# A hybrid decoder layer: another order of additions, weightings, splits and squares around the norm ahead of w_up

## The chip, the cores and the metric

The kernel runs on one core of one Trainium2 chip. A core has TensorE (PE, matrix products into PSUM), VectorE (DVE), ScalarE (ACT), GpSimd (POOL) and SyncE (SP, which here only issues DMAs); each runs its own instructions in order, and semaphores tie them together. The metric is the device time of one execution in microseconds (us). Before the change it is 1495.16 us, the median of three runs (1495.01 to 1495.42).

## The reference, cut to what matters

One decoder layer on 256 tokens of width 2048, in float32. Only the second half of the first residual and the start of the MLP are touched:

```
mix = hybrid_mixer(rmsnorm(h, norm_mix_pre), ...)      # ends in  y_mix @ w_out
h   = h + rmsnorm(mix, norm_mix_post)
ff  = squared_relu_mlp(rmsnorm(h, norm_mlp_pre), w_up, w_down)
h   = h + rmsnorm(ff, norm_mlp_post)

rmsnorm(x, w)               = x * rsqrt(mean(x * x) + EPS) * w
squared_relu_mlp(u, wu, wd) = (relu(u @ wu) ** 2) @ wd
```

## The kernel before, in words

**Precision.** Every float32 operand of a product is split into a high part `hi`, rounded on ScalarE, and a low part `lo`, the rest, on VectorE (`split`, L135, with its two instructions L138 and L139). A product is then three matmuls: high by high, high by low, low by high (L815 to L817).

**Tiles.** Tokens stand in two tiles of 128, t = 0 and 1. Output columns go in blocks of 512. A unit of work covers two column blocks, b = 0 and 1, and so four PSUM accumulators. Weights come in groups: a `Group` (L774) holds two blocks of 128 rows by 1024 columns, fetched by SyncE (L784) into `raw` (four buffers) or `raw_p` (two), split into `hi`/`lo` (five buffers, `hl_tiles`, L665) or, each sixth time, `hi_p`/`lo_p`. `plain` (L808) multiplies a group: six matmuls for each row block and token tile. `advance` (L843) keeps fetching two groups and splitting ahead of the matmuls. Other groups (`seven`, L819) use seven products instead of eight and need sums of blocks of the activations: `sums` (L710) builds them on VectorE (L707 to L715) and splits them.

**Order.** From L922 on the order is written out by hand: each engine does its work in the order of the code.

**The stretch around the norm.** The last unit of w_out ends with three groups, `x_`, `y_`, `z_`, whose products are done first for token tile 0, then for tile 1. The residual and the norms are worked in between, and the first three groups of w_up, `g0`, `g1`, `g2` (`lead`), fill TensorE. The fourth group of w_up (called `g3` in the text) is the first one of the loop at L1082. In this stretch:

- `final(r, acc, t, b)` (L885, VectorE) completes a block of `mix`: `r0[t, b]` holds columns 0 and 1, `r1[t, b]` columns 2 and 3.
- `squared` (L891, ScalarE) squares it, and sums the squares into `ssq`.
- `weighted(r, n)` (L894, VectorE) multiplies by the norm's weights, in place, after the square has read the block.
- `scale_of(rm, t, ...)` gathers the sums (L903, L905, VectorE) and takes the power -0.5 on GpSimd (L906) into `rm`, the tile `rmix` of the profile.
- `last_of(t, b)` (L993) calls these for `r1`. For b = 1 the weighting is a multiplication on GpSimd (L1000).
- `sum_up(t, n)` (L966, VectorE) is the addition `h = h + r * rm` for block n of tile t; I write it (t,n). For n = 0, 1 the profile shows it as `m<-r,rmix,m`, for n = 2, 3 as `m<-m,rmix`.
- `turn(t, n)` (L972, TensorE) transposes four 128x128 pieces of that block into PSUM.
- `split_turned(t, n)` copies them with the weights of the MLP norm on ScalarE (L978, four instructions), casts (L980) and takes the rest (L981) on VectorE. The result is the activation of two groups of w_up: block 0 feeds g0 and g1, block 1 feeds g2 and g3, and so on. Its scratch `v` comes from `strip` (tag `uu`, two buffers), as that of `sums` and of `square_sums` does.
- `square_sums(t)` (L983) squares the four blocks of `h` on ScalarE (L985), reduces (L987, L989, VectorE), takes the power on GpSimd (L990) into `rmlp`, and stores `h` to memory from GpSimd's queue (L991).

The 1/rms of the MLP norm is not applied before the products but after them: `up_end` (L1066) scales by `rmlp` when a unit of w_up is complete. The stored `h` is read back in the last unit of w_down (`load_h`, L947).

Of the kernel before, what the change touches and what calls it, by code (L numbers as in the profile page):

```python
# [19 lines left out]
NT = S // P  # L20
# [22 lines left out]
AHEAD = 1_000_000  # L43
BUFS = 5
EARLY = 5
LATE = 3
# [25 lines left out]
def hymba_layer(ctx: ExitStack, tc: tile.TileContext, x, norm_mix_pre, w_in, conv_w, conv_b, dt_bias, a_log,  # L72
                d_skip, ssm_norm_w, w_out, norm_mix_post, norm_mlp_pre, w_up, w_down, norm_mlp_post,
                consts, out):
    nc = tc.nc
# [76 lines left out]
    def parts():  # L152
        return [wp.tile([P, KB, NB], F32R, name=n, bufs=BUFS) for n in ("hi", "lo")]
# [415 lines left out]
    for hb in range(2):  # L569
# [4 lines left out]
        for xb in (2 * hb, 2 * hb + 1):  # L574
            xT = conv_block(COL_X + xb * NB, 4 * xb)
            z = gate_block(COL_Z + xb * NB)
            for j in range(2):
                g = 2 * xb + j
# [63 lines left out]
    rm = cp.tile([P, NT], F32, name="rmix")  # L642
# [3 lines left out]
    def columns(n):  # L646
        return slice(n * NB, (n + 1) * NB)
# [17 lines left out]
    def hl_tiles():  # L665
        turns["hl"] += 1
        if turns["hl"] % (BUFS + 1):
            return parts()
        return [pp.tile([P, KB, NB], F32R, name=n) for n in ("hi_p", "lo_p")]

    def strip(dtype=F32):
        return pp.tile([P, NB], dtype, name="uu", tag="uu", bufs=2)

    def quarters(t):
        return t.rearrange("p (i s) -> p i s", s=P)
# [95 lines left out]
    def aside():  # L771
        return [pp.tile([P, 3, NB], F32R, name=n) for n in ("xh", "xl")]
# [58 lines left out]
    groups = []  # L831

    def plan(src, n, kind, order):
        first = len(groups)
        groups.extend(Group(src, n, kind(abs(k)), by_seven) for k, by_seven in order)
        return range(first, len(groups))

    def order_of(ks, by_seven):
        return [(k, k in by_seven) for k in ks]
# [3 lines left out]
    def advance(to, sums=True):  # L843

        with tc.high_priority(offset=AHEAD):
            for what, last in (("fetch", to + 2), ("divide", to), ("add", to + 1), ("sums", to + 1)):
                while at[what] <= min(last, len(groups) - 1):
                    g = groups[at[what]]
                    if what == "divide" and at["add"] == at["divide"]:
                        g.add()  # L850
                        at["add"] += 1
                    if what == "sums":
                        if g.by_seven:
                            g.acts.sums()
                    else:
                        getattr(g, what)()
                    at[what] += 1

    def run(unit, acc, more, combine=None, hooks={}, to=None, started=False):

        sevens = [i for i in unit if groups[i].by_seven]
        for i in unit[:to]:
            advance(i + 2)
            if i in sevens:
                groups[i].seven(acc, more, i == sevens[0], i == sevens[-1])
            else:
                groups[i].plain(acc, first=i == unit[0] and not started, last=i == unit[-1])
            if sevens and i == sevens[-1]:
                combine(more)
            if i - unit[0] in hooks:  # L870
                hooks[i - unit[0]]()
# [12 lines left out]
    def final(r, acc, t, b):  # L884
        nc.vector.tensor_tensor(r[t, b], acc[b + 2 * t], r[t, b], op=ALU.subtract if b else ALU.add)  # L885

    def four():
        return {(t, b): pp.tile([P, NB], F32, name="r", bufs=4) for t in range(NT) for b in range(2)}

    def squared(r, acc, t, b, n):  # L890
        nc.scalar.activation(acc[b + 2 * t], r, AF.Square, accum_out=ssq[:, t, n:n + 1])  # L891

    def weighted(r, n):
        nc.vector.tensor_mul(r, r, wpost[:, n])  # L894
# [6 lines left out]
    def scale_of(dst, t, some):  # L901
        v = cp.tile([P, 1], F32, name="mean", bufs=2)
        nc.vector.tensor_scalar(v, ssq[:, t, 2:3], some, None, op0=ALU.add)  # L903
        m = cp.tile([P, 1], F32, name="mean", bufs=2)
        nc.vector.tensor_scalar(m, ssq[:, t, 3:4], v, 1.0 / D, op0=ALU.add, op1=ALU.mult)  # L905
        nc.gpsimd.tensor_tensor(dst[:, t:t + 1], m, half[:, 0:1], op=ALU.pow)  # L906

    def load_wpost(pool, src):
# [6 lines left out]
    up = [plan(w_up, 2 * n, Pre,  # L915
               order_of(range(8), ()) if n == 0 else
               order_of((0, 1, 3, 2, 5, 4, 7, 6), (3, 5, 7)) if n < 7 else
               order_of((0, 1, 3, 2, 5, 4, 6, 7), (3, 5))) for n in range(8)]
# [16 lines left out]
    some = {}  # L935
    run(wo0, acc, more, combined(r0), {len(wo0) - 1: first_end}, started=True)
    acc, more = more, acc
    r1 = {}
# [18 lines left out]
    wpost = None  # L957
# [6 lines left out]
    def sum_up(t, n):  # L964
        r = (r0, r1)[n // 2][t, n % 2]
        nc.vector.scalar_tensor_tensor(h[t][:, columns(n)], r, rm[:, t:t + 1], h[t][:, columns(n)],  # L966
                                       op0=ALU.mult, op1=ALU.add)

    def turn(t, n):
        for f in range(4):  # L970
            k = 4 * n + f
            nc.tensor.transpose(more[n][:, f * P:(f + 1) * P], h[t][:, k * P:(k + 1) * P], ident)  # L972

    def split_turned(t, n):
        v = quarters(strip())
        for f in range(4):
            k = 4 * n + f
            nc.scalar.activation(v[:, f], more[n][:, f * P:(f + 1) * P], AF.Copy, scale=w_mlp[:, k:k + 1])  # L978
        hi, lo = (us[n][:, :, i, t * P:(t + 1) * P] for i in range(2))
        nc.vector.tensor_copy(hi, v)  # L980
        nc.vector.tensor_tensor(lo, v, hi.bitcast(F32), op=ALU.subtract)  # L981

    def square_sums(t):  # L983
        for n in range(4):
            nc.scalar.activation(strip(BF16), h[t][:, columns(n)], AF.Square, accum_out=ssh[:, t, n:n + 1])  # L985
        v = cp.tile([P, 1], F32, name="some", bufs=4)
        nc.vector.tensor_reduce(v, ssh[:, t], axis=mybir.AxisListType.X, op=ALU.add)  # L987
        m = cp.tile([P, 1], F32, name="mean", bufs=2)
        nc.vector.tensor_scalar(m, v, D * EPS, 1.0 / D, op0=ALU.add, op1=ALU.mult)  # L989
        nc.gpsimd.tensor_tensor(rmlp[:, t:t + 1], m, half[:, 0:1], op=ALU.pow)  # L990
        nc.gpsimd.dma_start(hd[:, t], h[t])  # L991

    def last_of(t, b):  # L993
        final(r1, acc, t, b)
        squared(r1[t, b], acc, t, b, 2 + b)
        if b == 0:
            weighted(r1[t, b], 2)
            return
        scale_of(rm, t, some[t])
        nc.gpsimd.tensor_mul(r1[t, b], r1[t, b], wpost[:, 3])  # L1000

    lead = up[0][:LATE]
    x_, y_, z_ = (groups[i] for i in late)
    g0, g1, g2 = (groups[i] for i in lead)
    advance(late[-1])
    with tc.high_priority(offset=AHEAD):
        g0.part(0, [v[:, 0:KB] for v in aside()])
    for b in range(2):
        for g in (x_, y_, z_):
            g.plain(acc, last=g is z_, ts=(0,), bs=(b,))  # L1010
        last_of(0, b)
    sum_up(0, 0)
    sum_up(0, 1)
    x_.plain(acc, ts=(1,))
    advance(lead[0])
    y_.plain(acc, ts=(1,))
    turn(0, 0)
    turn(0, 1)
    sum_up(0, 2)
    with tc.high_priority(offset=AHEAD):  # L1020
        g1.part(0, hl_tiles())
    split_turned(0, 0)
    z_.plain(acc, last=True, ts=(1,))
    advance(lead[1])
# [1 line left out]
    g0.plain(acc, first=True, ts=(0,))  # L1026
    for b in range(2):
        last_of(1, b)
    turn(0, 2)
    g1.plain(acc, ts=(0,))  # L1030
    sum_up(0, 3)
    sum_up(1, 0)
    sum_up(1, 1)
    turn(1, 0)
    with tc.high_priority(offset=AHEAD):
        g2.part(0, hl_tiles())
    split_turned(1, 0)
    turn(1, 1)
    turn(0, 3)
    split_turned(0, 2)  # L1040
    g0.plain(acc, first=True, ts=(1,))
    split_turned(1, 1)
# [1 line left out]
    sum_up(1, 2)  # L1044
    g1.plain(acc, ts=(1,))
    turn(1, 2)
    split_turned(0, 3)
    sum_up(1, 3)
    g2.plain(acc, ts=(0,))
    turn(1, 3)  # L1050
    split_turned(1, 2)
    g2.plain(acc, ts=(1,))
    split_turned(1, 3)
    for t in range(NT):
        square_sums(t)

    ending = deque()

    def up_end(r, acc, n):

        def end():
            for t in range(NT):
                for b in range(2):
                    if n:
                        final(r, acc, t, b)
                    nc.scalar.activation(r[t, b], r[t, b] if n else acc[b + 2 * t], AF.Relu, scale=rmlp[:, t:t + 1])  # L1066
                    nc.scalar.activation(r[t, b], r[t, b], AF.Square)
            ending.append((r, acc, n))
        return end
# [12 lines left out]
    for n in range(8):  # L1082
        r = four()
        unit = up[n] if n else up[0][LATE:]
        hooks = {len(unit) - 1: up_end(r, acc, n)}
        if n:
            hooks[1] = turned
        else:
            hooks.update({i: Pre(k).sums for i, k in ((0, 3), (1, 5), (2, 7))})
        run(unit, acc, more, combined(r), hooks, started=n == 0)  # L1090
        acc, more = more, acc

# [63 lines left out]
```

## Time and profile before

| what | value |
|---|---|
| median of three runs | 1495.16 us (1495.01 to 1495.42) |
| the profiled execution's own time | 1493.86 us |
| its span | 1491.8 us |
| its mean granted TensorE clock | 0.995 |
| stretch from 758 to 900 us: TensorE busy | 133.69 of 142.00 us, clock 0.98 |
| stretch from 500 to 700 us: TensorE busy | 199.12 of 200.00 us, clock 1.00 |
| stretch from 900 to 1300 us: TensorE busy | 400.00 of 400.00 us, clock 1.00 |
| DMA | 287.28 MB, mean 193 GB/s |

The span runs from the first to the last instruction of the profiled execution; its own time has 2.1 us more around it. A row of a timeline gives the start, the duration, the engine, the line, the operation, the tiles (out<-in), the shapes and the count, and in brackets the idle time before it with what ended that. Rows of matmuls overlap: they are pipelined, so their starts tell the pace, not their durations. `PEld` is TensorE's loading of weights, `issue` a wait that the profile can't attribute.

### The profile page before, as it was taken

How to read it: one execution, taken by the hardware profiler on the slowest of the kernel's cores; microseconds unless marked ns; L12 is line 12 of the kernel's file. 1: busy time of each engine (PE TensorE's matmuls, PEld its weight loads, DVE VectorE, ACT ScalarE, POOL GpSimd, SP SyncE). 2: the span in 40 equal slices, each digit the busy share in tenths (PEclk: the TensorE clock that was granted, in tenths of full speed). 3: DMA queues.
4: the chain of work that ended last, by engine and by line, in shares of the span. 5: the costliest groups of instructions: out<-in, count | busy, mean ns of one | idle time of the engine just before them, and what ended most of it. 6: DMA issues, size and time to landing. Idle time of an engine off the chain costs nothing. (4 is left out here: it accounts for less than half of the span.)

```text
span 1491.8 us, 19561 instructions
## 1 busy us (share of the span) xinstructions
PE 1471.1 (99%) x7229; PEld 1242.0 (83%) x7229; DVE 1157.7 (78%) x1609; ACT 845.2 (57%) x1138; POOL 54.1 (4%) x77
## 2 busy tenths in 40 slices
PE   9999999999999999999997999999999999999997
PEld 8888888888888888878885888888888888888886
DVE  6988897886555555597987778888887899779995
ACT  7574565455545454554556565676665665656462
POOL 0002100220000000000001000000000000000000
PEclk9999999999999999999999999999999999999998
DMA  7666666555656555555674555655555556657652
GB/s 270 203 201 181 182 185 186 182 169 169 175 167 182 169 170 176 190 169 205 247 238 176 187 176 211 211 186 187 197 182 193 199 196 216 221 186 259 219 188 96
DMA packets 108751, 287.28 MB, mean 193 GB/s; under 512 B 11392, under 2 KB 14320, under 8 KB 107632
## 3 DMA queue, kind: packets, MB, share of 16 engines
q1 hardware_dynamic: 103632, 272.37, 56.2%
q0 software_dynamic: 1152, 8.39, 1.6%
q10 hardware_dynamic: 3872, 5.28, 1.1%
q8 instruction: 56, 0.92, 0.3%
q14 instruction: 39, 0.32, 0.1%
HBM read 281.78 MB, written 4.23 MB: 192 GB/s over the span
## 5 line engine op out<-in xcount | busy, mean ns | idle before, releaser
L139 DVE TENSOR_TENSOR lo<-raw,hi 128x1024 fp32r<-128x1024 f32 (+1 forms) x367 | 447.9, 1224 | 181.6 <-ACT hi L138 180.8
L138 ACT ACTIVATE hi<-raw 128x1024 fp32r<-128x1024 f32 (+1 forms) x367 | 383.7, 1050 | 278.1 <-PE acc L221 108.5
L221 PE MATMUL acc<-q,hi 128*128 128x512 f32 x1024 | 283.3, 402 | 0.6 <-DVE q L141 0.6
L221 PEld LDWEIGHTS acc<-q,hi 128*128 128x128 f32 x1024 | 178.8, 189 | 27.3 <-DVE q L141 0.8
L817 PE MATMUL acc<-hi,q 128*128 128x512 f32 x472 | 183.7, 389 | 0.0
L815 PE MATMUL acc<-hi,q 128*128 128x512 f32 x472 | 183.6, 389 | 0.0
L816 PE MATMUL acc<-lo,q 128*128 128x512 f32 x472 | 183.6, 389 | 0.0
L224 PEld LDWEIGHTS acc<-q,lo 128*128 128x128 f32 x1024 | 152.9, 189 | 19.2
L224 PE MATMUL acc<-q,lo 128*128 128x256 f32 x1024 | 157.8, 281 | 0.0
L139 DVE TENSOR_TENSOR lo<-raw_p,hi 128x1024 fp32r<-128x1024 f32 x95 | 115.8, 1219 | 16.3 <-ACT hi L138 16.2
L138 ACT ACTIVATE hi<-raw_p 128x1024 fp32r<-128x1024 f32 x95 | 99.7, 1050 | 33.3 <-DVE raw_p L793 15.0
L816 PEld LDWEIGHTS acc<-lo,q 128*128 128x128 f32 x472 | 88.6, 188 | 18.5
L817 PEld LDWEIGHTS acc<-hi,q 128*128 128x128 f32 x472 | 88.6, 188 | 18.5
L815 PEld LDWEIGHTS acc<-hi,q 128*128 128x128 f32 x472 | 88.6, 188 | 18.3
L199 PE MATMUL acc<-hi,q 128*128 128x512 f32 x256 | 100.1, 391 | 0.0
L200 PE MATMUL acc<-lo,q 128*128 128x512 f32 x256 | 99.7, 389 | 0.0
L201 PE MATMUL acc<-hi,q 128*128 128x512 f32 x256 | 99.7, 389 | 0.0
L138 ACT ACTIVATE q<-uu 128x512 fp32r<-128x512 f32 x21 | 13.3, 632 | 132.9 <-DVE uu L715 132.9
L139 DVE TENSOR_TENSOR xl<-xr,xh 128x1536 fp32r<-128x1536 f32 x44 | 77.3, 1757 | 11.2 <-ACT xh L138 11.0
L138 ACT ACTIVATE xh<-xr 128x1536 fp32r<-128x1536 f32 x44 | 65.1, 1480 | 15.3 <-PE ps L829 7.5
L139 DVE TENSOR_TENSOR lo_p<-raw,hi_p 128x1024 fp32r<-128x1024 f32 x43 | 52.5, 1220 | 12.8 <-ACT hi_p L138 12.8
L815 PE MATMUL ps<-hi,q 128*128 128x512 f32 x152 | 59.5, 392 | 0.0
(361 smaller groups left out, 2565.3 us busy)
## 6 DMA issues: line engine op xcount, KB each, us to landing
raw<-in_w_in_dram SPq DMA_DIRECT2D x190, 512.0 KB, 3.6
raw<-in_w_up_dram SPq DMA_DIRECT2D x86, 512.0 KB, 4.5
raw<-in_w_down_dram SPq DMA_DIRECT2D x85, 512.0 KB, 5.1
raw<-in_w_out_dram SPq DMA_DIRECT2D x46, 512.0 KB, 4.0
raw_p<-in_w_down_dram SPq DMA_DIRECT2D x43, 512.0 KB, 5.1
raw_p<-in_w_up_dram SPq DMA_DIRECT2D x42, 512.0 KB, 4.6
raw_p<-in_w_out_dram SPq DMA_DIRECT2D x18, 512.0 KB, 5.1
bc<-acs_d ACTq DMA_DIRECT2D x8, 512.0 KB, 4.6
```

The source lines that it names most:

```text
L138: return (nc.scalar.activation(hi, src, AF.Copy), nc.vector.tensor_tensor(lo, src, hi.bitcast(F32), op=ALU.subtract))
L139: nc.vector.tensor_tensor(lo, src, hi.bitcast(F32), op=ALU.subtract))
L199: nc.tensor.matmul(acc[t], a_h[:, r, ts], hi[:, j], start=begin, stop=False)
L200: nc.tensor.matmul(acc[t], a_h[:, r, ts], lo[:, j], start=False, stop=False)
L201: nc.tensor.matmul(acc[t], a_l[:, r, ts], hi[:, j], start=False, stop=end)
L221: nc.tensor.matmul(acc[f], hi[:, j, f * P:(f + 1) * P], u(k0 + j), start=k0 + j == 0, stop=False, skip_group_check=True)
L224: nc.tensor.matmul(acc[f][:, 0], lo[:, j, f * P:(f + 1) * P], u(k0 + j)[:, 0], start=False, stop=k0 + j == NK - 1, skip_group_check=True)
L815: nc.tensor.matmul(a, a_h, hi[:, b], start=first and j == 0, stop=False)
L816: nc.tensor.matmul(a, a_h, lo[:, b], start=False, stop=False)
L817: nc.tensor.matmul(a, a_l, hi[:, b], start=False, stop=last and j == KB - 1)
```

## The change

All of it stands in the hand-written stretch. `last_of` now holds only the final and the square. The weighting of `r1[t, 1]` goes from GpSimd to VectorE: for tile 0 behind the split of g0's second half, for tile 1 far later, ahead of the addition (1,3). For tile 1 both finals and squares come ahead of the weighting and the scale; the additions (0,3), (1,0) and (1,1) move up in the code. The split of g2's first half goes behind the cast of block (1,0). The two splits of g3 go from the loop into the stretch, ahead of the blocks (1,2) and (1,3). `square_sums` goes from the stretch into the loop, tile 0 behind the second group there and tile 1 behind the third, each followed by `Pre(k).sums` as before.

```diff
@@ -993,11 +993,6 @@
     def last_of(t, b):
         final(r1, acc, t, b)
         squared(r1[t, b], acc, t, b, 2 + b)
-        if b == 0:
-            weighted(r1[t, b], 2)
-            return
-        scale_of(rm, t, some[t])
-        nc.gpsimd.tensor_mul(r1[t, b], r1[t, b], wpost[:, 3])
 
     lead = up[0][:LATE]
     x_, y_, z_ = (groups[i] for i in late)
@@ -1005,20 +1000,27 @@
     advance(late[-1])
     with tc.high_priority(offset=AHEAD):
         g0.part(0, [v[:, 0:KB] for v in aside()])
+    def ahead(g, j):
+        with tc.high_priority(offset=AHEAD):
+            g.part(j, hl_tiles())
+
     for b in range(2):
         for g in (x_, y_, z_):
             g.plain(acc, last=g is z_, ts=(0,), bs=(b,))
         last_of(0, b)
+        if b == 0:
+            weighted(r1[0, 0], 2)
+    scale_of(rm, 0, some[0])
     sum_up(0, 0)
     sum_up(0, 1)
     x_.plain(acc, ts=(1,))
     advance(lead[0])
+    weighted(r1[0, 1], 3)
     y_.plain(acc, ts=(1,))
     turn(0, 0)
     turn(0, 1)
     sum_up(0, 2)
-    with tc.high_priority(offset=AHEAD):
-        g1.part(0, hl_tiles())
+    ahead(g1, 0)
     split_turned(0, 0)
     z_.plain(acc, last=True, ts=(1,))
     advance(lead[1])
@@ -1026,17 +1028,18 @@
     g0.plain(acc, first=True, ts=(0,))
     for b in range(2):
         last_of(1, b)
+    weighted(r1[1, 0], 2)
+    scale_of(rm, 1, some[1])
+    sum_up(0, 3)
+    sum_up(1, 0)
     turn(0, 2)
     g1.plain(acc, ts=(0,))
-    sum_up(0, 3)
-    sum_up(1, 0)
+    turn(1, 0)
     sum_up(1, 1)
-    turn(1, 0)
-    with tc.high_priority(offset=AHEAD):
-        g2.part(0, hl_tiles())
+    turn(1, 1)
     split_turned(1, 0)
-    turn(1, 1)
     turn(0, 3)
+    ahead(g2, 0)
     split_turned(0, 2)
     g0.plain(acc, first=True, ts=(1,))
     split_turned(1, 1)
@@ -1044,15 +1047,17 @@
     sum_up(1, 2)
     g1.plain(acc, ts=(1,))
     turn(1, 2)
+    weighted(r1[1, 1], 3)
+    sum_up(1, 3)
     split_turned(0, 3)
-    sum_up(1, 3)
     g2.plain(acc, ts=(0,))
     turn(1, 3)
+    g3 = groups[up[0][LATE]]
+    ahead(g3, 0)
     split_turned(1, 2)
+    ahead(g3, 1)
     g2.plain(acc, ts=(1,))
     split_turned(1, 3)
-    for t in range(NT):
-        square_sums(t)
 
     ending = deque()
 
@@ -1086,7 +1091,8 @@
         if n:
             hooks[1] = turned
         else:
-            hooks.update({i: Pre(k).sums for i, k in ((0, 3), (1, 5), (2, 7))})
+            hooks.update({0: Pre(3).sums, 1: lambda: (square_sums(0), Pre(5).sums()),
+                          2: lambda: (square_sums(1), Pre(7).sums())})
         run(unit, acc, more, combined(r), hooks, started=n == 0)
         acc, more = more, acc
```

VectorE, around the sums of squares of the second token tile (L885 is the final, L894 the weighting, L903 and L905 the sums, L966 the additions, L980 and L981 the cast and the rest, L139 a split of weights), as the difference of the two orders:

```order
 L885 TENSOR_TENSOR m<-ps,m 128x512
+L885 TENSOR_TENSOR m<-acc,m 128x512
 L894 TENSOR_TENSOR m<-m 128x512
-L885 TENSOR_TENSOR m<-acc,m 128x512
 L903 TENSOR_SCALAR mean<-ssq,some 128x1
 L905 TENSOR_SCALAR mean<-ssq,mean 128x1
 L966 SCALAR_TENSOR_TENSOR m<-m,rmix 128x512
 L966 SCALAR_TENSOR_TENSOR m<-r,rmix,m 128x512 x2
+L980 CAST q<-uu 128x4x128
+L981 TENSOR_TENSOR q<-uu,q 128x4x128
 L139 TENSOR_TENSOR lo<-raw,hi 128x1024
```

The second final stands ahead of the first weighting, and the cast and the rest of block (1,0) ahead of the split of g2.

ScalarE, from the last two squares of `r1` to the first difference for `seven` (L978 are the copies of transposed blocks, L985 the squares for the MLP norm, L138 splits, `m<-uu` that of a difference), before the change:

```order
L891 ACTIVATE acc,ssq<-m 128x512
L138 ACTIVATE hi<-raw 128x1024
L978 ACTIVATE uu<-acc,par 128x128 x12
L138 ACTIVATE hi<-raw_p 128x1024
L978 ACTIVATE uu<-acc,par 128x128 x12
L985 ACTIVATE uu,ssh<-m 128x512 x8
L138 ACTIVATE hi_p<-raw 128x1024
L138 ACTIVATE hi<-raw 128x1024
L138 ACTIVATE hi<-raw_p 128x1024
```

The same engine from the same instruction on, with the change:

```order
L891 ACTIVATE acc,ssq<-m 128x512
L978 ACTIVATE uu<-acc,par 128x128 x4
L138 ACTIVATE hi<-raw 128x1024
L978 ACTIVATE uu<-acc,par 128x128 x8
L138 ACTIVATE hi<-raw_p 128x1024
L978 ACTIVATE uu<-acc,par 128x128 x4
L138 ACTIVATE hi_p<-raw 128x1024
L978 ACTIVATE uu<-acc,par 128x128 x4
L138 ACTIVATE hi<-raw 128x1024
L978 ACTIVATE uu<-acc,par 128x128 x4
L138 ACTIVATE hi<-raw_p 128x1024
```

The eight squares are gone from this place, and g3's splits (`hi_p`, then `hi`) stand between the copies. And the squares' new place on ScalarE, with the change:

```order
L138 ACTIVATE m<-uu 128x512
L138 ACTIVATE hi_p<-raw 128x1024
L138 ACTIVATE hi<-raw 128x1024
L985 ACTIVATE uu,ssh<-m 128x512 x4
L138 ACTIVATE m<-uu 128x512
L138 ACTIVATE hi<-raw_p 128x1024
L138 ACTIVATE hi<-raw 128x1024
L985 ACTIVATE uu,ssh<-m 128x512 x4
L138 ACTIVATE m<-uu 128x512
```

Four squares follow each of two pairs of splits and precede the split of a difference. The orders of TensorE's and of SyncE's instructions are the same as before.

## The prediction

> **What bounds the kernel now.** I read the page first, then TensorE's waits, then the stages around them, then the timelines there. On the page, a row gives an engine's busy time, its share and its instructions.
>
> ```profile
> PE 1471.1 (99%) x7229; PEld 1242.0 (83%) x7229; DVE 1157.7 (78%) x1609; ACT 845.2 (57%) x1138; POOL 54.1 (4%) x77
> ```
>
> TensorE is the bound, and its work does not change. Only its gaps and its clock can be won. Its two longest waits (total, times, longest):
>
> ```profile
> PE ps L815 <- ACT hi_p L138: 4.5, 1, 4.5
> PE acc L972 <- DVE m L966: 2.7, 1, 2.7
> ```
>
> Both lie in the edited stretch. I call the 2.7 wait A and the 4.5 wait B. The windows around them give busy times, granted clock and DMA:
>
> ```profile
> 787.00:794.00 7.00, 3.64 (x20) 2.56 (x20) 6.15 (x8) 3.77 (x14) 2.10 (x2) 1.00 0.20 60
> 804.40:815.10 10.70, 5.75 (x13) 4.09 (x13) 6.73 (x10) 9.30 (x18) 2.22 (x4) 0.69 0.68 253
> ```
>
> Around A the clock stays at 1.00; after B it falls to 0.69, so B costs more than its length. B on TensorE, and what comes behind it:
>
> ```profile
> 803.91 0.39 PE L816 MATMUL acc<-lo,q 128*128 128x512 f32 x1
> 804.14 0.39 PE L817 MATMUL acc<-hi,q 128*128 128x512 f32 x1
> 809.01 0.79 PE L815 MATMUL ps<-hi_p,q 128*128 128x512 f32 x1 [4.48 <-ACT hi_p L138]
> ```
>
> ```profile
> 815.13 0.50 PE L815 MATMUL ps<-hi,q 128*128 128x512 f32 x1
> ```
>
> Starts are 0.23 apart. The last matmul of g2 starts at 804.14; the first twelve of g3 would take 2.76, so g3's second half would begin at 804.37 + 2.76 = 807.13. It begins at 815.13: **B costs 8.0 us**, wait and slow matmuls together. What ScalarE did meanwhile, and when SyncE issued g3's two loads:
>
> ```profile
> 802.85 0.65 ACT L985 ACTIVATE uu<-m 128x512 bf16<-128x512 f32 x1
> ...
> 807.92 1.04 ACT L138 ACTIVATE hi_p<-raw 128x1024 fp32r<-128x1024 f32 x1
> ```
>
> ```profile
> 767.41 10.99 SPq L784 DMA_DIRECT2D raw<-in_w_up_dram  x2
> DMA to landing us min/median/max: 3.5/5.0/6.2
> ```
>
> Eight squares fill ScalarE from 802.85 to 807.92 (0.63 each), and g3's split comes next in its order. The data were issued by 778.40 and landed by 784.6 at the latest. So B is ScalarE's order, not data.
>
> **The change, squares and fourth group.** The eight squares leave this place, and both splits of g3 go ahead of the transposed blocks (1,2) and (1,3). The splits need only the data and a free buffer, whose last reader (g0's matmuls on the second tile) ends near 792.5. I put `hi_p` at about 795 and both `lo` parts before 801, while TensorE reaches g3 at about 802. B goes whole: **8.0**. The two added VectorE splits there stand beside TensorE's matmuls of g1 and g2; if that cover fails, B comes back in part.
>
> What is late next are the squares in their new place. Rows of VectorE in a later group, with a split and the four-step difference (L707 to L715) and its split:
>
> ```profile
> 820.44 1.22 DVE L139 TENSOR_TENSOR lo<-raw,hi 128x1024 fp32r<-128x1024 f32 x1
> 821.58 0.69 DVE L707 TENSOR_TENSOR uu<-q 128x512 f32<-128x512 f32 x1
> ...
> 824.08 0.69 DVE L139 TENSOR_TENSOR m<-uu,m 128x512 fp32r<-128x512 f32 x1 [0.70 <-ACT m L138]
> ```
>
> In each of two groups ScalarE now runs in series: two splits (estimate 2 x 0.95, the 1.04 row overlapping its successor), four squares (4 x 0.63 = 2.5), a wait for the reduction and mean on VectorE (estimate 0.4), and a wait for the difference with its own split (821.58 to 824.08, 2.5): 7.3 us against TensorE's 24 x 0.23 = 5.5. It loses 1.8 twice. I put the splits of g6 at 812, while TensorE needs them three groups after 802, at 818.5: a lead of 6.5, of which about 2.9 stays for the group behind g7. The scale `rmlp`, wanted at the end of g7 near 829, is there by 821. Cost of the move: **0**, hidden by that lead. The stores of `h` on GpSimd's queue move with the squares; nobody reads them before the last weight block.
>
> **The change, second tile's chain (A).**
>
> ```profile
> 786.65 0.39 PE L817 MATMUL acc<-hi,q 128*128 128x512 f32 x1
> 789.71 1.82 PE L972 MATMUL acc<-cst,m 128*128 128x128 f32 x12 [2.67 <-DVE m L966]
> 792.12 0.50 PE L815 MATMUL ps<-xh,q 128*128 128x512 f32 x1 [0.59 <-DVE q L980]
> ```
>
> TensorE is free at 786.88, transposes at 789.71, and goes on with g0 at 792.12. The chain behind it, on VectorE, ScalarE and GpSimd:
>
> ```profile
> 783.02 0.68 DVE L885 TENSOR_TENSOR m<-ps,m 128x512 f32<-128x512 f32 x1
> 784.50 0.69 DVE L894 TENSOR_TENSOR m<-m 128x512 f32<-128x512 f32 x1 [0.79 <-ACT ps L891]
> 785.11 0.68 DVE L885 TENSOR_TENSOR m<-acc,m 128x512 f32<-128x512 f32 x1
> 785.71 0.20 DVE L903 TENSOR_SCALAR mean<-ssq,some 128x1 f32<-128x1 f32 x1
> 786.58 0.21 DVE L905 TENSOR_SCALAR mean<-ssq,mean 128x1 f32<-128x1 f32 x1 [0.67 <-ACT acc L891]
> 786.71 0.74 DVE L966 SCALAR_TENSOR_TENSOR m<-m,rmix 128x512 f32<-128x512 f32 x1
> 787.91 1.75 DVE L966 SCALAR_TENSOR_TENSOR m<-r,rmix,m 128x512 f32<-128x512 f32 x1 [0.45 <-POOL rmix L906]
> ```
>
> ```profile
> 783.74 0.60 ACT L891 ACTIVATE ps<-m 128x512 f32<-128x512 f32 x1 [2.65 <-DVE m L885]
> ```
>
> ```profile
> 773.87 0.57 POOL L906 TENSOR_TENSOR rmix<-mean,half 128x1 f32<-128x1 f32 x1 [24.76 <-DVE mean L905]
> 774.41 1.28 POOL L1000 TENSOR_TENSOR m<-m 128x512 f32<-128x512 f32 x1
> 786.88 0.99 POOL L906 TENSOR_TENSOR rmix<-mean,half 128x1 f32<-128x1 f32 x1 [11.18 <-DVE mean L905]
> 787.85 1.25 POOL L1000 TENSOR_TENSOR m<-m 128x512 f32<-128x512 f32 x1
> ```
>
> ```profile
> L966 DVE SCALAR_TENSOR_TENSOR m<-r,rmix,m x4: 737/1242/1780, 774.5 to 789.6; 128x512 f32<-128x512 f32 x4
> ```
>
> - **GpSimd's multiplication goes.** The same addition takes 0.74 or, in the two cases where GpSimd multiplies beside it (774.41 and 787.85), 1.78 and 1.75. Each such addition becomes 1.0 shorter. In the first tile VectorE gets that 1.04 back and pays 0.61 (784.50 to 785.11) for the weighting that is put there: it reaches the second tile's first final (783.02) about 0.4 earlier, at 782.6.
> - **Both finals first.** The second final runs at 783.2. The first square starts 0.72 after its final, at 783.3, the second at about 784.05 when ScalarE is free. The first weighting needs the first square (0.76 from start to start): 784.07. L903 follows at 784.7, L905 at about 785.0 (its square is ready by 784.8, 0.75 after its start, as 785.83 to 786.58 would have it). That is 1.6 before 786.58.
> - **The scale and the addition.** GpSimd starts 0.3 after L905 and took 0.99 or 0.57. Which value? VectorE's (0,3) addition runs beside it again, as at 786.71, so I take the nearer row, 0.99, and keep 0.57 as the good end (0.4 less). The addition (1,0) starts at 786.3, ends at 787.05 instead of 789.66: 1.6 + 1.0 = **2.6 earlier**.
>
> [...]
>
> From the first transpose to TensorE's next matmul nothing is shortened, so 2.41 stays (789.71 to 792.12):
>
> ```profile
> 790.47 2.18 ACT L978 ACTIVATE uu<-acc,par 128x128 f32<-128x128 f32 x8 [2.97 <-PE acc L972]
> ```
>
> ```profile
> 791.64 0.43 DVE L980 CAST q<-uu 128x512 fp32r<-128x512 f32 x1 [0.19 <-ACT uu L978]
> ```
>
> TensorE transposes at 787.1, the first copies follow 0.76 later, the cast at 789.0, g0 at 789.5. ScalarE's split of g2 moves behind those copies and VectorE's behind the cast, so nothing new stands ahead. **A gives 2.6**; TensorE keeps a wait of about 0.2 and one of about 1.2.
>
> A margin follows:
>
> ```profile
> 797.98 0.60 PE L972 MATMUL acc<-cst,m 128*128 128x128 f32 x4
> 798.33 0.48 PE L815 MATMUL ps<-hi,q 128*128 128x512 f32 x1
> ```
>
> The block (1,2), transposed at 797.98, would come at 795.4. VectorE reaches its addition after three pairs of cast and rest (estimate 1.07 each) and two splits (1.14 each, 820.44 to 821.58) from 789.0: 794.5, done at 795.2. It fits by 0.2; missing it costs tenths. The second tile's last weighting (0.61) now follows it on VectorE, ahead of the addition (1,3): done by 796.5, while block (1,3) is transposed three microseconds after (1,2), hence nothing.
>
> **Sum.** 8.0 + 2.6 = 10.6. The profiled execution took 1493.86 (span 1491.8), 1.3 under the median of 1495.16; the gain is in the span, so I take it off both: 1483.3 for a profiled run like it and **1484.6** for the median. The best end: of A, 792.12 - 786.88 = 5.24 less twelve transposes (four take 0.35) leaves 4.2; 8.0 + 4.2 = 12.2 gives 1483.0.
>
> **Rivals.**
> - *The slow addition is not GpSimd's doing* (its place after a wait, say). Then VectorE comes 1.0 later and the addition stays 1.0 longer: 1484.6 + 2.0 = 1486.6. The row's minimum of 0.74 for the same form speaks against it. Chance 0.06.
> - *The waits left in A let the clock fall.* Twelve matmuls would take 0.43 instead of 0.23 each, as behind B: +2.4, 1487.0. Against it: around A, with TensorE busy 3.64 of 7.00, the clock was 1.00. [...] Chance 0.05.
> - *B does not go*: g3's split waits for something the ScalarE rows hide, a buffer or data that came at 807.9 by chance. Only A is won: 1492.6, within 0.2% (about what a measurement of this kernel can tell from no change). The load rows speak against it. Chance 0.05.
> - *Slower: the squares' chain starves the later groups.* Its place is g6 to the group behind g7. If the cycle of 7.3 became about 13 (the two `uu` buffers, shared by squares and differences, making the engines take turns), the lead of 2.9 would go and two waits of about 4.5 follow, each with 2.4 of slow matmuls: 13.8 back against 10.6 won, 1498.4. It decides on this side from a cycle of 13; the counted steps give 7.3. Chance 0.04.
>
> **How the numbers follow.** The forecast has 0.80. The range runs from 1482.7 (the best end less 0.3 of scatter) to 1487.2 (both first rivals within it). Faster by over 0.2% sums the forecast and the first two rivals: 0.91; same 0.05; slower 0.04.
>
> **What would show it.** Right: no wait of TensorE on `hi_p` at g3, clock 1.00 through the stretch, all additions at 0.74, no multiplication on GpSimd, the (1,0) addition near 786.3, TensorE waits of about 0.2 and 1.2 there, no new wait between g6 and the first block behind g7. Wrong: a wait for L138 or L139 after g5, a slow clock near 790, or an addition (1,0) of 1.75 with GpSimd quiet.

## The result and the profile after

The changed kernel takes 1483.76 us, the median of four runs (1482.85 to 1484.39), against 1495.10 us (1495.01 to 1495.42): the ratio is 0.9923, with a 95% interval from 0.9906 to 0.9941. That is 11.3 us less; the forecast was 10.6 less, 1484.6, in a range from 1482.7 to 1487.2. The profiled execution took 1484.39 (span 1482.2).

TensorE's waits in the profile after, all of them (total, times, longest):

```profile
PE ps L380 <- DVE dg L379: 1.2, 1, 1.2
PE ps L272 <- DVE half L261: 1.1, 1, 1.1
PE acc L221 <- DVE q L141: 1.0, 1, 1.0
PE acc L827 <- ACT q L138: 0.9, 1, 0.9
PE ps L815 <- DVE q L980: 0.6, 1, 0.6
PE ps L448 <- DVE dA L443: 0.2, 1, 0.2
```

A (L972 for the addition) and B (`hi_p`, `lo_p`) are gone from the list. In the windows that showed them before, TensorE is busy 6.23 of 7.00 and 10.70 of 10.70 us, and the clock, the third number from the end, is 1.00 in both:

```profile
787.00:794.00 7.00, 6.23 (x31) 4.37 (x30) 5.13 (x9) 4.99 (x15) 0.41 (x1) 1.00 0.08 16
804.40:815.10 10.70, 10.70 (x49) 8.87 (x48) 8.57 (x13) 5.98 (x13) 0.12 (x1) 1.00 0.80 270
```

Absolute times of two profiles can't be compared here: this execution comes to the stretch later, by about the wait of 1.2 at L380, 47 us after its start, in code that the change does not touch. So I measure **the stretch**, from the first final of tile 0 to the first matmul of g3's second half. Before, the final stood at 768.01 (VectorE):

```profile
768.01 0.69 DVE L885 TENSOR_TENSOR m<-ps,m 128x512 f32<-128x512 f32 x1 [0.63 <-PE ps L817]
```

and the matmul at 815.13: 47.12 us. After, by the rows of VectorE and TensorE,

```profile
769.13 0.69 DVE L885 TENSOR_TENSOR m<-ps,m 128x512 f32<-128x512 f32 x1 [0.63 <-PE ps L817]
```

```profile
805.66 0.39 PE L815 MATMUL ps<-hi,q 128*128 128x512 f32 x1
```

it is **36.53, 10.59 us shorter**. To compare rows, take 769.13 - 768.01 = 1.12 off the times after. TensorE around A, after:

```profile
787.78 0.39 PE L817 MATMUL acc<-hi,q 128*128 128x512 f32 x1
788.26 1.82 PE L972 MATMUL acc<-cst,m 128*128 128x128 f32 x12
790.66 0.50 PE L815 MATMUL ps<-xh,q 128*128 128x512 f32 x1 [0.59 <-DVE q L980]
```

The transposes start at 787.14 in the times of before, 2.57 ahead of 789.71. The chain behind them on VectorE and GpSimd, after:

```profile
783.73 0.68 DVE L885 TENSOR_TENSOR m<-ps,m 128x512 f32<-128x512 f32 x1
784.33 0.68 DVE L885 TENSOR_TENSOR m<-acc,m 128x512 f32<-128x512 f32 x1
785.20 0.69 DVE L894 TENSOR_TENSOR m<-m 128x512 f32<-128x512 f32 x1 [0.19 <-ACT ps L891]
785.81 0.21 DVE L903 TENSOR_SCALAR mean<-ssq,some 128x1 f32<-128x1 f32 x1
786.12 0.22 DVE L905 TENSOR_SCALAR mean<-ssq,mean 128x1 f32<-128x1 f32 x1
786.26 0.74 DVE L966 SCALAR_TENSOR_TENSOR m<-m,rmix 128x512 f32<-128x512 f32 x1
787.45 1.42 DVE L966 SCALAR_TENSOR_TENSOR m<-r,rmix,m 128x512 f32<-128x512 f32 x2 [0.45 <-POOL rmix L906]
```

```profile
774.99 0.57 POOL L906 TENSOR_TENSOR rmix<-mean,half 128x1 f32<-128x1 f32 x1 [24.76 <-DVE mean L905]
786.42 0.99 POOL L906 TENSOR_TENSOR rmix<-mean,half 128x1 f32<-128x1 f32 x1 [10.86 <-DVE mean L905]
```

The two additions (1,0) and (1,1) take 1.42 together, where they took 2.41. GpSimd only takes the two powers in this stretch, the second one again in 0.99. On ScalarE, the first splits of g3 and, later, the first squares of either tile, after:

```profile
794.91 1.18 ACT L138 ACTIVATE hi_p<-raw 128x1024 fp32r<-128x1024 f32 x1
...
811.97 0.61 ACT L985 ACTIVATE uu<-m 128x512 bf16<-128x512 f32 x1
...
819.08 0.61 ACT L985 ACTIVATE uu<-m 128x512 bf16<-128x512 f32 x1
```

The split that came at 807.92 comes at 794.91 (793.79 in the times of before), and the first squares of the two tiles start 7.1 us apart in the loop.

### The profile page after: what moved, and what is told of

Same layout as the page of the kernel before. It is cut to its first block, busy times and chain, and to the rows that moved or that the text cites. A ratio compares the mean times of both kernels' runs of the same rounds, so it can differ in the third digit from the quotient of the medians.

```text
span 1482.2 us, 19558 instructions
## 1 busy us (share of the span) xinstructions
PE 1467.6 (99%) x7229; PEld 1239.7 (84%) x7229; DVE 1156.6 (78%) x1611; ACT 844.5 (57%) x1138; POOL 52.2 (4%) x75
## 4 chain that ended last, share of the span: by engine, by line
PE 94%; DVE 2%; DMA 1%; issue 1%; ACT 1%; SPq 0%; POOL 0%; POOLq 0%; DVEq 0%; ACTq 0%
PE acc L221 15%; PE acc L817 10%; PE acc L815 10%; PE acc L816 10%; PE acc L224 7%; PE acc L199 4%; PE acc L201 4%; PE acc L200 4%; PE ps L815 3%; PE ps L817 3%; PE ps L816 3%; PE acc L827 3%; PE acc L829 3%; PE acc L828 3%; PE ps L829 1%; PE ps L827 1%
## 5 line engine op out<-in xcount | busy, mean ns | idle before, releaser
L139 DVE TENSOR_TENSOR lo<-raw,hi 128x1024 fp32r<-128x1024 f32 (+1 forms) x367 | 447.8, 1224 | 177.8 <-ACT hi L138 177.2
L138 ACT ACTIVATE hi<-raw 128x1024 fp32r<-128x1024 f32 (+1 forms) x367 | 383.8, 1050 | 275.3 <-PE acc L221 107.5
L139 DVE TENSOR_TENSOR lo<-raw_p,hi 128x1024 fp32r<-128x1024 f32 x95 | 115.9, 1219 | 16.3 <-ACT hi L138 16.2
L138 ACT ACTIVATE hi<-raw_p 128x1024 fp32r<-128x1024 f32 x95 | 99.9, 1052 | 33.3 <-DVE raw_p L793 15.0
L138 ACT ACTIVATE q<-uu 128x512 fp32r<-128x512 f32 x21 | 13.3, 632 | 132.9 <-DVE uu L715 132.9
L139 DVE TENSOR_TENSOR xl<-xr,xh 128x1536 fp32r<-128x1536 f32 x44 | 77.3, 1757 | 11.2 <-ACT xh L138 10.9
L138 ACT ACTIVATE xh<-xr 128x1536 fp32r<-128x1536 f32 x44 | 65.1, 1480 | 15.3 <-PE ps L829 7.4
L139 DVE TENSOR_TENSOR lo_p<-raw,hi_p 128x1024 fp32r<-128x1024 f32 x43 | 52.4, 1220 | 12.1 <-ACT hi_p L138 12.1
```

The costliest lines, as they stand in the source:

```text
L138: return (nc.scalar.activation(hi, src, AF.Copy), nc.vector.tensor_tensor(lo, src, hi.bitcast(F32), op=ALU.subtract))
L139: nc.vector.tensor_tensor(lo, src, hi.bitcast(F32), op=ALU.subtract))
```

## The experiments

The forecast came out; three things were still only argued: which part of the change wins what, that GpSimd's reading made the addition slow, and what the clock adds. Twelve runs followed, three of them of the two kernels as they are. Unless said otherwise a number below is the stretch of one profile, 47.12 before and 36.53 after.

**Squares alone.** The kernel before, with this edit:

```diff
-    for t in range(NT):
-        square_sums(t)
...
-            hooks.update({i: Pre(k).sums for i, k in ((0, 3), (1, 5), (2, 7))})
+            hooks.update({0: Pre(3).sums, 1: lambda: (square_sums(0), Pre(5).sums()),
+                          2: lambda: (square_sums(1), Pre(7).sums())})
```

> The kernel before with the squares for the MLP norm moved into the loop, and nothing else. I measure the stretch from the first final of tile 0 to the first matmul of g3's second half: 47.1 us before, 36.5 with the whole change. Theory (B is ScalarE's order and the clock that falls behind it): g3's split follows the copies of block (1,3) at once, hi_p is ready about 0.4 before TensorE wants it, lo_p about 0.6 late; wait B shrinks to some 0.6, the clock stays at 1.00, wait A stays at 2.7. Stretch 39.7, time 7.4 us less than before. Rival (the early splits carry the gain, the squares alone only move the wait): TensorE still waits 2 us or more at g3, the time falls by less than 5.

The stretch is 40.46 (768.49 to 808.95), the time 1488.76 against 1495.33 (ratio 0.9959, 0.9944 to 0.9974): 6.6 less. B is one wait of 0.6 for `lo_p`, as the theory has it:

```profile
806.30 0.50 PE L816 MATMUL ps<-lo_p,q 128*128 128x512 f32 x1 [0.61 <-DVE lo_p L139]
```

The stretch is 0.8 longer than expected; 0.44 of it lies behind A, where the clock fell (below).

**Early splits alone.** The kernel before, with this edit:

```diff
     turn(1, 3)
+    g3 = groups[up[0][LATE]]
+    with tc.high_priority(offset=AHEAD):
+        g3.part(0, hl_tiles())
     split_turned(1, 2)
+    with tc.high_priority(offset=AHEAD):
+        g3.part(1, hl_tiles())
     g2.plain(acc, ts=(1,))
```

> The kernel before with the two splits of g3 moved ahead of the copies of blocks (1,2) and (1,3), the squares left where they were. Theory: g3 finds its weights, B goes; the squares then end about 807.9 and g4's split follows, which TensorE wants at 809.8: hi on time, lo about 0.2 late. Stretch 39.1, time 7.8 us less than before. So either part alone would win most of the 8.0, and they do not add. Rival (the eight squares are the cause, wherever the split of g3 stands): the wait moves to g4, 3 us or more, and the time falls by less than 5.

39.70 (768.62 to 808.32), and 1487.72 against 1495.33 (0.9953, 0.9936 to 0.9969): 7.6 less. There is no wait at g3. At g4, behind the end of the stretch, the loading of weights waits 0.51 for `lo`, where 0.2 was expected. Rows of TensorE in this run, the first matmuls of g3 and of its second half, and that wait:

```profile
805.60 0.39 PE L815 MATMUL ps<-hi_p,q 128*128 128x512 f32 x1
...
808.32 0.39 PE L815 MATMUL ps<-hi,q 128*128 128x512 f32 x1
```

```profile
811.52 0.19 PEld L816 LDWEIGHTS ps<-lo,q 128*128 128x128 f32 x1 [0.51 <-DVE lo L139]
```

Six matmuls from 811.04 on take 1.77 there instead of 1.36, so 0.4 is lost that the stretch does not count. What is over the expected 39.1 is again the clock behind A: from the transposes there to those of block (1,2) it takes 8.84 instead of 8.27. Less that 0.57 the stretch is 39.13, and 47.12 less the 8.02 that B is worth (below) is 39.10. So **the early splits alone remove all of B in the stretch and lose 0.4 at g4; the squares alone remove all but 0.9** (40.46 less 0.44 is 40.02). What B needed was that eight squares and g3's split should not stand in this order in front of TensorE's demand.

**Half the squares.** The kernel before, with `square_sums(0)` left in its place and `square_sums(1)` moved into the loop.

> The kernel before with only tile 1's four squares moved into the loop; tile 0's stay ahead of g3's split. Theory (part of B is the clock, which falls only behind a long wait): hi_p comes 2.0 us late and lo_p another 1.0; the clock stays at 1.00; B costs 3.1 instead of 8.0, stretch 42.2. Rival 1 (the clock falls behind a wait of 2 to 3 us as well): 5.5, stretch 44.6. Rival 2 (the cost goes with the number of squares): 4.0, stretch 43.1.

45.16 (769.31 to 814.47). Rival 1 came out, my theory did not. B on TensorE in this run:

```profile
808.35 0.69 PE L815 MATMUL ps<-hi_p,q 128*128 128x512 f32 x1 [2.04 <-ACT hi_p L138]
809.61 0.80 PE L816 MATMUL ps<-lo_p,q 128*128 128x512 f32 x1 [0.57 <-DVE lo_p L139]
810.20 0.63 PE L817 MATMUL ps<-hi_p,q 128*128 128x512 f32 x1
810.63 0.63 PE L815 MATMUL acc<-hi_p,q 128*128 128x512 f32 x1
```

The waits are the expected ones, 2.04 and 0.57, but the matmuls behind start 0.43 apart, not 0.23. Here a wait of 2.04 and a short one behind it brought a slow clock too (0.50 from 810 to 813 us), in one profile. About half of the waiting (2.6 of 4.95) left most of the cost: 45.16 less 0.44 for A's clock is 44.72, which saves 2.4 of 8.0.

**The clock behind A.** In these three kernels, which are the same as before up to A, TensorE's twelve transposes behind A took 2.6 to 2.7 us, though the wait was 2.66, 2.67 before, where they took 1.82; the clock from 792 to 795 us was 0.71, 0.57 and 0.53, and 1.00 before. That asked for the unchanged kernel again, twice.

> The kernel before, unchanged, profiled once more. In its first profile the clock stayed at 1.00 behind wait A (2.67); in three kernels that are the same up to that place it fell, and the transposes took 2.6 to 2.7 instead of 1.8. Theory (whether a wait of 2.7 lets the clock fall differs between executions of one program): in at least one of two further profiles the transposes take about 2.7 and the stretch up to the transposes of (1,2) is 30.4 to 30.6 instead of 30.0. Rival (it belongs to the program): the clock stays at 1.00 there both times.

> The same as the run ahead of it, a third profile of the kernel before: theory, the transposes behind wait A take about 2.7 in some executions and 1.8 in others; rival, always 1.8.

The transposes of the first of these runs, then of the second:

```profile
789.64 1.82 PE L972 MATMUL acc<-cst,m 128*128 128x128 f32 x12 [2.67 <-DVE m L966]
```

```profile
791.18 2.82 PE L972 MATMUL acc<-cst,m 128*128 128x128 f32 x12 [2.67 <-DVE m L966]
```

And two windows of the second run, with the clock as the third number from the end:

```profile
789.00:792.00 3.00, 0.82 (x4) 0.81 (x5) 2.62 (x3) 0.00 (x0) 1.57 (x2) 0.79 0.00 0
792.00:795.00 3.00, 2.95 (x13) 2.16 (x12) 2.32 (x4) 2.34 (x9) 0.00 (x0) 0.64 0.35 66
```

The first stretch is 47.12 (767.94 to 815.06), the second 47.60 (769.49 to 817.09). The clock is 0.79 and 0.64 there, and 1.00 in the same windows of the first run. One program, one wait of 2.67, and the clock falls in one execution and stays in another. What decides it no run here shows. A wait of 2.66 or 2.67 was enough in four of the six profiles that have it at A, and so were the waits of 2.04 and 0.57 above. Behind B's 4.5 the clock fell each time, in four profiles (to between 0.50 and 0.70 from 810 to 813 us); in the seven whose longest wait in the stretch was 1.25 or less it never did (1.00 from 786 to 798 and from 804 to 813 us in each).

**Weightings alone.** The kernel before, with this edit:

```diff
         scale_of(rm, t, some[t])
-        nc.gpsimd.tensor_mul(r1[t, b], r1[t, b], wpost[:, 3])
...
     advance(lead[0])
+    weighted(r1[0, 1], 3)
     y_.plain(acc, ts=(1,))
...
-    split_turned(0, 3)
-    sum_up(1, 3)
+    weighted(r1[1, 1], 3)
+    sum_up(1, 3)
+    split_turned(0, 3)
```

> The kernel before with the two weightings moved from GpSimd to VectorE, to the places that the change gives them, and nothing else. Theory (the addition beside GpSimd's multiplication takes 1.75 for 0.74): all additions take 0.74, the second tile's first final starts 0.4 earlier, wait A falls from 2.7 to about 1.3, B stays at 4.5 with a slow clock behind it. Stretch 45.7, time 1.4 us less than before, a hair over what can be measured. Rival (the slow addition is slow for another reason, such as being the first one after a wait): additions (0,0) and (1,0) stay at 1.75, VectorE is later by 0.6, stretch 47.7.

45.72 (768.46 to 814.18), 1.40 less, as expected; A is 1.24, B stays 4.48:

```profile
788.74 1.82 PE L972 MATMUL acc<-cst,m 128*128 128x128 f32 x12 [1.24 <-DVE m L966]
```

All additions take 0.74 or 0.75. The time, 1492.83 against 1495.33 in ten runs (0.9983, 0.9974 to 0.9992), is 2.5 less, by the interval 1.2 to 3.9, so that the 1.4 lies within it. That the shorter A no longer risks the clock may be a part of the rest; it is not shown.

**The old order of the finals.** The changed kernel, with this edit:

```diff
-    for b in range(2):
-        last_of(1, b)
-    weighted(r1[1, 0], 2)
+    last_of(1, 0)
+    weighted(r1[1, 0], 2)
+    last_of(1, 1)
```

> The changed kernel with the second tile's first weighting put back between the two finals, as before. Theory (finals first let the second square start while VectorE weights): L905 comes 1.2 us later, so does the addition (1,0), and TensorE waits about 1.2 longer ahead of the transposes. Stretch 37.7 against 36.5. Rival (the wait for the copies and the cast behind the transposes hides it): stretch 36.5.

37.71 (769.33 to 807.04): 1.18 more than the change, with a wait of 1.25 ahead of the transposes:

```profile
789.61 1.82 PE L972 MATMUL acc<-cst,m 128*128 128x128 f32 x12 [1.25 <-DVE m L966]
```

With the weightings' 1.40 that makes 2.58, the whole of A's gain.

**GpSimd beside the addition.** The changed kernel, with one line behind `scale_of(rm, 1, some[1])`, a multiplication in one run and a memset in the other:

```diff
+    nc.gpsimd.tensor_mul(wpost[:, 0], wpost[:, 0], wpost[:, 1])
```

```diff
+    nc.gpsimd.memset(wpost[:, 0], 0.0)
```

> The changed kernel with a multiplication on GpSimd added right behind the power of tile 1, of two blocks that nobody reads any more, as large as the one that the change removes (it changes no result). Theory (two engines stand in each other's way when both read SBUF): the addition (1,0) takes 1.7 to 1.8 instead of 0.74, TensorE's transposes come 1.0 later, stretch 37.5. Rival (the slow addition comes from what it waits for or reads itself): it stays at 0.74, stretch 36.5.

> The same with a memset of that block on GpSimd in place of the multiplication: GpSimd writes as much and reads nothing. Theory (it is GpSimd's reading that is in the way): the addition (1,0) stays at 0.74, stretch 36.5. Rival (any work of GpSimd on SBUF is in the way): it takes over 1.2, stretch 37 or more.

The addition (1,0) and GpSimd's work with the multiplication:

```profile
786.30 1.77 DVE L966 SCALAR_TENSOR_TENSOR m<-r,rmix,m 128x512 f32<-128x512 f32 x1 [0.45 <-POOL rmix L906]
```

```profile
786.24 1.27 POOL L1033 TENSOR_TENSOR m<-m 128x512 f32<-128x512 f32 x1
```

and with the memset:

```profile
789.37 0.75 DVE L966 SCALAR_TENSOR_TENSOR m<-r,rmix,m 128x512 f32<-128x512 f32 x1 [0.45 <-POOL rmix L906]
```

```profile
789.30 0.52 POOL L1033 MEMSET m<- 128x512 f32 x1
```

The stretches are 37.59 (767.98 to 805.57) and 36.52 (771.06 to 807.58). A multiplication of blocks that the addition never touches costs it 1.0 us; a memset that overlaps it for 0.45 costs nothing. That points to GpSimd's reading, though the two also differ in length (1.27 against 0.52) and in what they compute. The multiplication started 0.06 earlier, and the addition ends 0.56 after it (788.07 against 787.51), as if it had waited for most of it. Had the memset, which ends at 789.82, blocked it in that way, it would have taken about 1.0 (an estimate: 789.82 + 0.56 - 789.37).

**A version that fills the wait left in A.** The changed kernel, with this edit (hi-first products of g2 on tile 0 where TensorE waits for the cast; `second_part` is what remains of `g2.plain`):

```diff
     turn(1, 1)
+    ahead(g2, 0)
     split_turned(1, 0)
     turn(0, 3)
-    ahead(g2, 0)
+    first_part(g2, 0)
     split_turned(0, 2)
...
-    g2.plain(acc, ts=(0,))
+    second_part(g2, 0)
...
+    def first_part(g, t):
+        (hi, lo), (a_h, a_l) = g.hl[0], g.acts.block(0, t)
+        for a_, w_ in ((a_h, hi), (a_l, hi), (a_h, lo)):
+            for b in range(2):
+                nc.tensor.matmul(acc[b + 2 * t], a_, w_[:, b], start=False, stop=False)
```

> The changed kernel with six matmuls of g2 on tile 0 taken out of their place and put behind the twelve transposes, high parts first, where TensorE waits about 1.3 us for the cast of block (1,0); g2's split goes back ahead of that cast, into a gap of VectorE of 1.3 us. Theory (that wait is the last one left in the stretch): it goes, and the one of 0.2 on the rest (L981) stays. Stretch 35.2, 1.3 us less than the changed kernel. Rival (the split of 1.14 on VectorE delays the cast as much as it fills): stretch 36.5 or more.

35.38 (767.89 to 803.27), 1.15 less than the change, a little short of the expected 1.3; the profile lists no wait of TensorE's matmuls in the stretch. VectorE's split of g2 fits its gap; rows of VectorE in this run:

```profile
787.54 1.22 DVE L139 TENSOR_TENSOR lo<-raw,hi 128x1024 fp32r<-128x1024 f32 x1
788.95 0.43 DVE L980 CAST q<-uu 128x512 fp32r<-128x512 f32 x1 [0.19 <-ACT uu L978]
```

The time was 1482.96 (1481.74 to 1484.16; ratio to before 0.9927, 0.9913 to 0.9941), which can't be told from the changed kernel's. Both ran again on one chip.

> The changed kernel once more, beside the version with the filled wait on the same chip. Theory: stretch 36.5 again, whatever the start of the run costs; time 10.6 to 11.6 below before. Rival (part of the gain was the luck of one profile): stretch over 37.

> The version with the filled wait, beside the changed kernel. Theory: stretch 35.4 again and a median about 1.1 below the changed kernel's. Rival (given back behind the stretch): stretch 35.4, and a median within 0.5 of the changed kernel's.

The changed kernel: 36.54 (768.61 to 805.15), median 1483.71 in five runs (0.9926, 0.9912 to 0.9939). The filled one: 35.36 (772.02 to 807.38), median 1482.49 in four (0.9918, 0.9905 to 0.9932). The stretch is shorter by 1.18, the medians by 1.2, but the single times overlap (1483.30 to 1485.25, and 1481.47 to 1485.80): the profiles show the gain twice, the times alone do not settle it.

## Why the prediction was right, point by point

- **B, 8.0.** Right: 10.59 less A's 2.57 is 8.02. That it was ScalarE's order and not data is shown, since reordering alone (early splits) removes it. The steps came too: in the times of before `hi_p` starts at 793.8 (about 795 forecast), the two `lo` parts end at 798.9 and 801.1 (before 801), and TensorE reaches g3 at 801.8 (about 802). What I did not say is that the early splits alone bring all of it but 0.4, and the squares' move alone all but 0.9.
- **A, 2.6.** Right, 2.57, and so were the steps: in the times of before the first final starts at 782.61 (782.6 forecast), the second at 783.21 (783.2), L905 at 785.00 (785.0), the addition (1,0) at 786.33 (786.3), the transposes at 787.14 (787.1), g0 at 789.54 (789.5). For the power the nearer row, 0.99, was the one to take. From the first transpose to g0 it takes 2.40 (2.41 before), as forecast, though the profile lists only 0.59 of that as a wait, not 1.2; filling it won 1.15.
- **GpSimd in the addition's way.** Right; the rival, that the addition is slow on its own, fell with the idle multiplication.
- **The squares cost nothing in the loop.** Right: a cycle of 7.1 (7.3 forecast). The first split behind g7 ends on VectorE at 826.6, some 3.5 before TensorE reaches it at 830.1, so the lead was a little larger than the 2.9 forecast. The scale `rmlp` is there at 821.9 in the times of before, not by 821, but ScalarE, its first reader, still waits 0.2 for TensorE at the end of the unit. The rival of starved groups did not come.
- **The margin at block (1,2).** Right and thin: forecast 795.4, in fact 795.42.
- **The clock.** My ground against the second rival was the row of one profile, a clock of 1.00 around A. It was too strong, and that this one profile had kept its clock was luck: the same wait did let it fall in another execution of that kernel and in three kernels that are the same up to there. So waits like the old A are not harmless. That the rival did not come fits the shorter waits that A keeps: all eight profiles with 1.25 or less there kept the clock, four of the six with 2.66 or 2.67 did not. Over the whole stretch of the changed kernel (769.13 to 805.66) the clock is 1.00. What the rival would have cost, 2.4, was too high for A: 0.4 to 0.6 were measured, as most of the slow time fell on the transposes and on a wait. In the executions where it fell, A was thus worth about 3.0.
- **The sum and the median.** The stretch gave 10.59 for 10.6. The profiled execution was 1.1 above my 1483.3 for it, by the 1.12 with which it came to the stretch. The median fell 11.3, and 11.7 in the repetition: 0.7 to 1.1 more than the sum. A part is the slow clock in the kernel before. From the first final of tile 0 to the end of the span its three profiles take 723.8, 723.9 and 724.6, the two of the changed kernel 713.1 and 713.1: 10.7 to 11.5 less. The longest is the execution whose clock fell behind A (0.4); behind B, too, its matmuls stayed slow for longer (from the first one behind the stretch to the fourth 1.14, against 0.80 and 0.88), so that it has 677.0 behind the stretch, the other two 676.7, and those of the changed kernel 676.5. What is left of the 11.3 and 11.7 would lie ahead of the stretch, where single executions of the filled version alone differ by four microseconds (767.89 and 772.02). It was not pinned down.

## What to carry to other kernels

Where TensorE is the bound, as here (99% busy), a wait in front of it costs about its length (a wait of 1.25 cost 1.18 with the old order of the finals) and, behind the waits of 2.04 to 4.5 here, in some executions a slow clock on top; removing about half of the waiting left 5.6 of its cost of 8.0, as half the squares showed. Work that nobody waits for yet belongs behind the last split that the next matmul wants, and moving that split ahead won nearly all of it here. A helper engine can slow the engine that it relieves: the multiplication moved off VectorE saved it 0.6 and cost the addition beside it 1.0 (1.75 for 0.74), and one of blocks that the addition never touches cost it as much (1.77); a memset did not (0.75).

## What was not expected of the hardware

- The clock is a matter of the single execution: behind one wait of 2.67 us in one program, twelve transposes took 1.82 and 1.82, and in a third execution 2.82.
- GpSimd's power on 128 numbers takes 0.57 alone and 0.99 beside a VectorE addition; in the loop, beside the difference L707, `rmlp` took 0.92 and 0.93 where it had been 0.54 and 0.56. `rmlp` is ready at 823.02 and first read at 828.36, so there this costs nothing.
